# A hybrid decoder layer on one core: a hand-interleaved program is replaced by a recorded program that a list scheduler in the kernel's source lays out

## The chip, the core and the metric

The kernel runs on one core of a Trainium2 chip. The metric is device time of one execution in microseconds (us); less is better. The kernel before takes 591.33 us (median of three runs, 591.09 to 591.43).

A core has engines that each work through their own queue of instructions in order: TensorE (PE in the profile; its weight loads are PEld), VectorE (DVE), ScalarE (ACT), GpSimd (POOL), and SyncE (SP), which here issues all DMA transfers. They are tied together by semaphores. Matmuls write to PSUM, which has eight banks of 128 x 512 fp32; everything else lies in SBUF.

## The reference

One decoder layer, 1024 tokens of width 1024. The normed input is projected to 3584 columns that are split among eight stick-breaking attention heads (q, k, v), two blocks of a gated short convolution, four heads that attend to 256 memory tokens, and a gate over the whole mixing width.

```python
h = _rmsnorm(x, g_in); proj = h @ w_in
# stick-breaking: A[t,s] = sigmoid(z_ts) * prod_{s<j<t} (1 - sigmoid(z_tj))
z = einsum('bqhd,bkhd->bhqk', q_blk, k) * scale
log_not = where(before, log_sigmoid(-z), 0.0)
suffix = cumsum(log_not, axis=3, reverse=True) - log_not
w = where(before, exp(log_sigmoid(z) + suffix), 0.0)
y_sb = einsum('bhqk,bkhd->bqhd', w, v)
y_conv = b_c * causal_conv3(c_c * u_c)
y_mem = softmax(q_mem @ mk.T * scale) @ mv        # mk, mv from the normed memory
y = concatenate([_rmsnorm(y_sb), _rmsnorm(y_conv), _rmsnorm(y_mem)])
out = _rmsnorm(x + (y * silu(gate)) @ w_out)
```

## The kernel before, in words

Precision comes from splitting: each fp32 operand is written as a high part (`whi`, `xh`, `wth`, `q`) and a rest (`wlo`, `xl`, `wtl`, `qs`), and each product takes three (or two) fast matmuls. A split costs one cast and one subtraction.

**Start.** Lines 170 to 209 load x by chunks of 128 input channels, split it, and compute v of all heads in all eight PSUM banks at once (192 matmuls of 128 x 512). The row norms come out of the rows of x; v is copied to `vh`.

**Background work.** `proj` (line 267) projects one block of 128 columns: 48 matmuls of 128 x 512, 24 into each of two `pj` banks, one bank after the other, with a yield after every three. There are 24 such blocks, with the k and q of each head pair, the convolution, the memory queries and eight gates, and `mem_kv` (line 643) with 48 more matmuls. Weights come through one raw buffer `wraw` and two buffers each of `whi` and `wlo` (`load_w`, line 132): a DMA, two casts on ACT or DVE by the letters of `WENG`, two subtractions on POOL.

**A stick-breaking head.** Its queries are taken in four stages of 256 (`sp`). `sb_scores` (line 366) makes a block of scores z, takes two sigmoids of it on ACT (F, the chance of not breaking, and sg), runs a product scan over F on DVE (lines 387 and 389), and multiplies sg by F on DVE or POOL, as the letter of `MENG` says for that head (line 392): heads 0, 4, 5 and 7 on POOL, the others on DVE. `transposed` (line 331) transposes the weights on PE, casts them on ACT (`wth`, line 340) and subtracts on DVE (`wtl`, line 341); line 416 multiplies by v; `put_y` adds the halves. A head pair uses one q and one k projection (`qk`, two buffers). A memory head (`mem_unit`, line 508) has two such stages with a softmax in place of the scan.

**Order.** `attention` (line 681) lists the steps of six stick-breaking heads, then the four memory heads, then the last two stick-breaking heads. `run` (line 699) walks through them and, after each, advances the background until its time is the step's times a factor from `RATIO`; the order of the background is the string `BG` (line 50). `behind_attention` ties each third background matmul behind an attention step some places back. The program that comes out is ordered once more by the compiler's own scheduler, with a simulation of time.

**End.** The last gate (`proj_last`, line 251) uses the `z` banks. Then 8 blocks of 128 rows go through the output projection (line 789), three groups of PSUM pairs per block; the sum, the norm and the store follow on DVE, ACT and POOL.

Of the kernel before, what the change touches and what calls it, by code (L numbers as in the profile page):

```python
# [12 lines left out]

# [40 lines left out]
def hymba_kernel(ctx, tc, xT, xr, wp, wv, memT, memr, wmem, cols, eye, wout, gfin, out):  # L54
    nc = tc.nc
    PSUM = bass.MemoryType.PSUM

# [4 lines left out]
    vyp = ctx.enter_context(tc.tile_pool(name="vyp", bufs=1))
    ps_pj = ctx.enter_context(tc.tile_pool(name="ps_pj", bufs=PJ_BUFS, space=PSUM))
    ps_z = ctx.enter_context(tc.tile_pool(name="ps_z", bufs=2, space=PSUM))
    ps_tr = ctx.enter_context(tc.tile_pool(name="ps_tr", bufs=TR_BUFS, space=PSUM))
    ps_av = ctx.enter_context(tc.tile_pool(name="ps_av", bufs=2, space=PSUM))

    dram = ctx.enter_context(tc.tile_pool(name="dram", bufs=1, space=bass.MemoryType.DRAM))
    row = dram.tile([TB, P], F32, name="row")

    uid = [0]

    def nm(s):
        uid[0] += 1
        return f"{s}_{uid[0]}"

    def pj_tile():
        return ps_pj.tile([P, H], F32, tag="pj", name=nm("pj"))

    def z_tile():  # L80
        return ps_z.tile([P, H], F32, tag="z", name=nm("z"))

    def tr_tile():
        return ps_tr.tile([P, H], F32, tag="tr", name=nm("tr"))

    def av_tile(full=False):
        t = ps_av.tile([P, H], F32, tag="av", name=nm("av"))
        return t if full else t[:, 0:256]

    def stage(shape=None, dt=F32):  # L90
        return stg.tile(shape or [P, H], dt, tag="stg", name=nm("stg"))

    def slot(n, shape, dt, name):
        return vyp.tile(shape, dt, tag=f"s{n}", name=nm(name))
# [5 lines left out]
    col = const.tile([P, 32], F32, name="col")  # L100
# [9 lines left out]
    nhalf = const.tile([P, 8], F32, name="nhalf")  # L110
    nc.vector.memset(nhalf, -0.5)
    ones = const.tile([P, 2], F32R, name="ones")
    onesf = const.tile([P, 2], F32, name="onesf")
    nc.vector.memset(onesf, 1.0)
    nc.vector.tensor_copy(ones, onesf)
    rstd = const.tile([P, TB], F32, name="rstd")
    rq = const.tile([P, TB], F32, name="rq")
    nrq = const.tile([P, TB], F32, name="nrq")
    rb = const.tile([P, T], F32, name="rb")
    rstdm = const.tile([P, 2], F32, name="rstdm")  # L120
    rg = const.tile([P, 3, TB], F32, name="rg")
    sums = const.tile([P, TB], F32, name="sums")
    sumsm = const.tile([P, 2, 2], F32, name="sumsm")
    gsum = [const.tile([P, TB], F32, name=f"gsum{g}") for g in range(3)]

# [730 lines left out]
```

## Time and profile before

| | us |
|---|---|
| median of three runs | 591.33 |
| the profiled execution, its own time | 591.88 |
| its span on the core | 590.1 |
| start to the first score matmul of head 0 | 74.9 |
| heads 0 to 4 (to the first score matmul of head 5) | 178.1 |
| head 5 and the four memory heads | 107.2 |
| heads 6 and 7, last gates (to the first output matmul) | 133.8 |
| output projection to the last matmul | 89.7 |
| after the last matmul | 6.4 |

The profiled execution spends 1.8 us outside the span. The profile has a page (busy time of each engine, the chain of work that ended last, the costliest groups) and views of the trace: groups of instructions, stretches of time with each engine's busy time, and instructions in order of time. A matmul's end is modelled: it shows 0.39 us long although the next starts 0.23 us after it, so PE's busy share overstates its work; starts are the better measure.

### The profile page before, as it was taken

The page shows a single profiled execution, that of the slowest core. Times are in us where ns is not written, and L with a number is a line of the kernel's source. Part 1 is how long each engine was busy: PE and PEld are TensorE (multiplying, and loading weights), DVE is VectorE, ACT ScalarE, POOL GpSimd, SP SyncE. Part 2 cuts the span into 40 slices and gives each one's busy share as a digit, 9 for nine tenths or more (in the row PEclk, how much of TensorE's full clock was granted, in tenths as well). Part 3 has the DMA queues.
Part 4 walks back from the last instruction along what each step waited for, and adds up shares of the span by engine and source line. Part 5 has one row for each costly group of instructions (what it writes and reads, how often), then busy time and mean ns, then how long its engine had stood idle before and what let it go on. Part 6 is the DMA issues. An engine that isn't in the chain of part 4 may idle for free.

```text
span 590.1 us, 8309 instructions
## 1 busy us (share of the span) xinstructions
PE 556.6 (94%) x2776; PEld 460.2 (78%) x2776; DVE 426.6 (72%) x680; ACT 340.0 (58%) x743; POOL 300.5 (51%) x317
## 2 busy tenths in 40 slices
PE   8999999999899999978799999889988999999995
PEld 5888878878788888756688888778767878788884
DVE  3525039899999995779756858995887487977564
ACT  5747465657586686767556987554544464443332
POOL 2551586743134229987845667056876477301000
PEclk9999999999999999989899999889999999999999
DMA  8931421211312011232222221101001164132301
GB/s 284 403 137 38 116 64 36 73 37 36 108 37 72 24 49 37 55 90 72 71 83 66 69 72 36 37 36 37 30 7 36 37 252 142 37 142 103 113 37 71
DMA packets 22187, 48.36 MB, mean 82 GB/s; under 512 B 7808, under 2 KB 8320, under 8 KB 22144
## 3 DMA queue, kind: packets, MB, share of 16 engines
q1 hardware_dynamic: 22144, 47.82, 25.3%
q8 instruction: 22, 0.36, 0.2%
q14 instruction: 21, 0.17, 0.1%
HBM read 36.78 MB, written 4.20 MB: 69 GB/s over the span
## 4 chain that ended last, share of the span: by engine, by line
PE 32%; DVE 12%; issue 5%; ACT 3%; POOL 2%; DMA 2%; SPq 1%; POOLq 0%; DVEq 0%; ACTq 0%
PE pj L273 11%; PE tr L789 7%; PE pj L789 4%; PE z L789 3%; DVE wtl L341 2%; DVE F L389 2%; PE z L258 2%; DVE F L387 2%; PE tr L335 2%; PE av L416 1%; DMA part<-stg 1%; POOL sg L392 1%; PE z L527 1%; DVE whi L144 1%; DVE sg L392 1%
## 5 line engine op out<-in xcount | busy, mean ns | idle before, releaser
L273 PE MATMUL pj<-xh,whi 128*128 128x512 f32 x368 | 147.2, 400 | 1.0 <-DVE mv L668 1.0
L273 PE MATMUL pj<-xl,whi 128*128 128x512 f32 x368 | 145.1, 394 | 0.0
L273 PE MATMUL pj<-xh,wlo 128*128 128x512 f32 x368 | 145.1, 395 | 0.0
L145 POOL TENSOR_TENSOR wlo<-wraw,whi 128x512 fp32r<-128x512 f32 x56 | 82.6, 1491 | 26.3 <-ACT whi L142 12.9
L387 DVE TENSOR_TENSOR_SCAN F<-F,mask 128x513 f32<-128x513 f32 (+2 forms) x64 | 77.8, 1219 | 13.3 <-ACT F L384 10.0
L273 PEld LDWEIGHTS pj<-xh,wlo 128*128 128x128 f32 x368 | 69.3, 188 | 13.6
L273 PEld LDWEIGHTS pj<-xh,whi 128*128 128x128 f32 x368 | 69.4, 189 | 12.7 <-DVE mv L668 1.2
L273 PEld LDWEIGHTS pj<-xl,whi 128*128 128x128 f32 x368 | 69.6, 189 | 11.9
L392 POOL TENSOR_TENSOR sg<-sg,F 128x512 f32<-128x512 f32 (+3 forms) x48 | 62.2, 1298 | 27.6 <-DVE F L389 10.5
L384 ACT ACTIVATE F<-z,nrq 128x512 f32<-128x512 f32 (+3 forms) x96 | 56.1, 586 | 33.8 <-PE z L377 23.0
L341 DVE TENSOR_TENSOR wtl<-tr,wth 128x512 fp32r<-128x512 f32 (+1 forms) x96 | 59.7, 637 | 9.9 <-ACT wth L340 9.1
L385 ACT ACTIVATE sg<-z,rq 128x512 f32<-128x512 f32 (+2 forms) x96 | 55.7, 583 | 9.3 <-PE tr L335 9.2
L340 ACT CAST wth<-tr 128x512 fp32r<-128x512 f32 (+1 forms) x96 | 51.5, 555 | 14.9 <-PE tr L335 14.0
L416 PE MATMUL av<-wtl,vh 128*128 128x256 f32 (+1 forms) x160 | 43.3, 303 | 13.6 <-DVE wtl L341 13.5
L335 PE MATMUL tr<-ident,sg 128*128 128x128 f32 x288 | 48.3, 282 | 5.1 <-POOL sg L392 2.5
L383 POOL MEMSET F<- 128x1 f32 x96 | 9.8, 104 | 78.6 <-DVE F L389 38.8
L389 DVE TENSOR_TENSOR_SCAN F<-F,F,mask 128x512 f32<-128x512 f32 (+1 forms) x32 | 41.7, 1304 | 8.7 <-ACT F L384 6.4
L316 POOL TENSOR_TENSOR qs<-qk,q 64x512 fp32r<-64x512 f32 x24 | 32.7, 1377 | 28.7 <-ACT q L315 28.1
L416 PEld LDWEIGHTS av<-wtl,vh 128*128 128x128 f32 x160 | 31.3, 196 | 20.3 <-DVE wtl L341 18.0
L416 PE MATMUL av<-wth,vh 128*128 128x256 f32 (+1 forms) x160 | 45.1, 287 | 0.0
L801 POOL TENSOR_TENSOR ssf<-ssf,nhalf 128x1 f32<-128x1 f32 x8 | 7.4, 927 | 69.1 <-DVE ssf L798 59.8
L335 PEld LDWEIGHTS tr<-ident,sg 128*128 128x128 f32 x288 | 34.2, 144 | 9.2 <-POOL sg L392 3.9
(182 smaller groups left out, 1197.0 us busy)
## 6 DMA issues: line engine op xcount, KB each, us to landing
wraw<-in_wp SPq DMA_DIRECT2D x24, 512.0 KB, 3.3
xs<-in_xr SPq DMA_DIRECT2D x8, 512.0 KB, 7.9
wor<-in_wout SPq DMA_DIRECT2D x8, 512.0 KB, 4.9
acc<-in_xr SPq DMA_DIRECT2D x8, 512.0 KB, 3.8
out<-acc SPq DMA_DIRECT2D x16, 256.0 KB, 2.2
xs<-in_xT SPq DMA_DIRECT2D x7, 512.0 KB, 7.9
qs<-q SPq DMA_DIRECT2D x12, 256.0 KB, 2.9
q<-qs SPq DMA_DIRECT2D x12, 256.0 KB, 3.0
```

Source lines behind the costliest of these rows:

```text
L145: nc.gpsimd.tensor_tensor(lo[:, c], raw[:, c], f(hi[:, c]), op=ALU.subtract)
L273: ins = nc.tensor.matmul(ps, lhsT=ww[:, k, :], rhs=xx[k][:, hf], start=(k == 0 and a == 0), stop=(k == KC - 1 and a == 2))
L335: ins = nc.tensor.transpose(tr[:, i * P : (i + 1) * P], blk, ident)
L340: nc.scalar.copy(wh[:, 0:n], tr[:, 0:n])
L341: nc.vector.tensor_tensor(wl[:, 0:n], tr[:, 0:n], f(wh[:, 0:n]), op=ALU.subtract)
L384: nc.scalar.activation(F[:, 1:m], zz[:, 0 : m - 1], AF.Sigmoid, scale=nrq[:, i : i + 1])
L385: nc.scalar.activation(sg[:, c0:c1], zz, AF.Sigmoid, scale=rq[:, i : i + 1])
L387: nc.vector.tensor_tensor_scan(F[:, 0:m], F[:, 0:m], M[:, 0:m], 0.0, ALU.mult, ALU.max)
L389: nc.vector.tensor_tensor_scan(F[:, 0:m], F[:, 0:m], M[:, 130 : 130 + m], prev[:, H - lo : H - lo + 1], ALU.mult, ALU.max)
L392: eng.tensor_tensor(sg[:, c0:c1], sg[:, c0:c1], F[:, 0:w], op=ALU.mult)
L416: nc.tensor.matmul(av[:, 0 : c.stop - c.start], lhsT=key(j), rhs=w[:, c], start=(g == 0 and j == 1 and n == 0), stop=(g == ng - 1 and j == ...
L789: nc.tensor.matmul(ps[:, pc], lhsT=yy[:, c, :], rhs=ww[c][:, c0:c1], start=(c == cs[0] and a == 0), stop=(c == cs[-1] and a == 2))
```

## The change

Nothing of what is computed changes. The functions of the kernel no longer issue instructions: they record them in a `Plan`, which notes for each the tiles it reads and writes, so the instructions it must follow, and a priority. `lay_out` then plays the program on five engines with a table of costs, and at each moment gives every free engine the ready instruction of the lowest priority number whose tiles have room; `emit` issues them in that order, and the compiler's scheduler is switched off. Buffers of one tag are handed out in recorded order. Every instruction of the new program carries the line of the kernel's decorator, so its tiles tell them apart.

```diff
-WENG = 'vssssvvvsvvssvvsvvvssvvvvsss'
-MENG = 'pvvvppvp'
-KENG = 'ppvvvvvv'
-BG = 'qk1 c0 ms qk2 qm0 qm1 g0 kv qk3 g1 c1 g5 g7 g4 g6 g3 g2'
+COST = {"vector": (0.13, 0.00108), "scalar": (0.17, 0.00084), "gpsimd": (0.3, 0.0023)}
+LAG = {"tensor": 0.22, "vector": 0.1, "scalar": 0.1, "gpsimd": 0.12}
+PATIENCE = 6.0
...
+        def pick(e):
+            fits = [o for o in ready[e] if o.start is None and room(o)]
...
+            if e == "scalar":
+                same = [o for o in fits if o.table in (None, table)]
+                late = [o for o in fits if o.table not in (None, table) and now - o.ready > PATIENCE]
+                fits = late or same or fits
+            return min(fits, key=lambda o: (o.prio, o.n))
...
+    ATT, EVAC, SPLIT, FILL, POST = 1000.0, 300.0, 400.0, 5000.0, 20000.0
...
     def load_w(src, shape):
...
+            nc.scalar.copy(hi[:, c], raw[:, c], prio=SPLIT + fills[0])
+            nc.either.tensor_tensor(lo[:, c], raw[:, c], f(hi[:, c]), op=ALU.subtract, prio=SPLIT + fills[0])
...
+                nc.tensor.matmul(ps[i], lhsT=ww[:, k, :], rhs=xx[k][:, hf], start=first,
+                                 stop=(k == KC - 1 and a == 2), prio=FILL + fills[0] + (0 if both else 0.4 * i),
+                                 after=after if first else ())
...
-            eng = nc.vector if MENG[st["u"]] == "v" else nc.gpsimd
-            eng.tensor_tensor(sg[:, c0:c1], sg[:, c0:c1], F[:, 0:w], op=ALU.mult)
+            nc.either.tensor_tensor(sg[:, c0:c1], sg[:, c0:c1], F[:, 0:w], op=ALU.mult)
...
-    units = [(f"qk{p}", sb_unit(p, a, qk[p])) for p in range(3) for a in range(2)]
-    units += [("qm", mem_unit(h, qm, mkv)) for h in range(4)]
-    units += [("qk3", sb_unit(3, a, qk3)) for a in range(2)]
-    run(attention(units), bg, RATIO[0])
+    qk = [(q_proj(0), k_proj(4))]
+    pair(0, *qk[0])
+    qk.append((q_proj(1), k_proj(5)))
+    pair(1, *qk[1])
+    qk.append((q_proj(2), k_proj(6)))
+    conv(0)
+    pair(2, *qk[2])
+    qk.append((q_proj(3), k_proj(7)))
+    mk, mv = mem_kv()
+    stats(0, 0, True)
+    gate(0, (last[0],))
+    pair(3, *qk[3])
+    conv(1)
+    qm = [q_proj(14)]
+    mem_head(0, qm[0], mk, mv)
...
+    gate(6, (last[6],))
+    gate(7, (last[7],), both=True)
...
-    with tile.TileContext(nc, schedule_with_timeline_sim=True) as tc:
+    with tile.TileContext(nc) as tc:
```

`ATT` is the priority of attention (plus ten for each later head), `EVAC` that of emptying a projection's bank, `SPLIT` of splitting weights, `FILL` of projection matmuls, `POST` of the output. The lowest number goes first, so attention goes ahead of projections, and projections in recorded order take what is left. `either` lets VectorE or GpSimd take the instruction, whichever is free first. All eight stick-breaking heads now come before the memory heads. Pools, sizes and numbers of buffers are as before.

Three places show how instructions moved. On PE, at the start of head 5 of the kernel before (`z` scores, `av` times v, `tr` transposes, `pj` projections):

```order
L377 MATMUL z_2697<-k_2627,q_2619 128x512
L377 MATMUL z_2697<-k_2627,qs_2620 128x512
L416 MATMUL av_2539<-wth_2572,vh_464 128x256
L377 MATMUL z_2706<-k_2627,q_2619 128x512
L377 MATMUL z_2706<-k_2627,qs_2620 128x512
L416 MATMUL av_2539<-wtl_2573,vh_464 128x256
L416 MATMUL av_2539<-wth_2572,vh_464 128x256
L416 MATMUL av_2539<-wtl_2573,vh_464 128x256
L335 MATMUL tr_2653<-ident,sg_2503 128x128
L335 MATMUL tr_2653<-ident,sg_2579 128x128
```

The same place on PE after the change, in the first stage of head 5:

```order
L321 MATMUL z_2487<-k_2065,qs_2062 128x512
L321 MATMUL av_2367<-wtl_2478,vh_525 128x256
L321 MATMUL av_2508<-wth_2494,vh_525 128x256
L321 MATMUL pj_2388<-xl_241,whi_2140 128x512
L321 MATMUL pj_2514<-xh_160,whi_2328 128x512
L321 MATMUL av_2508<-wtl_2504,vh_525 128x256
L321 MATMUL pj_2388<-xh_232,wlo_2151 128x512
L321 MATMUL av_2508<-wth_2494,vh_525 128x128
L321 MATMUL tr_2526<-ident_151,sg_506_2420 128x128 x2
L321 MATMUL pj_2388<-xh_317,whi_2140 128x512
```

Before, the whole first stage of head 5 has no projection matmul; now they stand between the attention's, and the two banks of a block (here of two blocks) take turns.

On DVE before, in head 2, with the scans of F (shown under the name of their family, SCALAR_TENSOR_TENSOR) and the multiplies of sg:

```order
L389 SCALAR_TENSOR_TENSOR F_1480<-F_1480,F_1471,mask 128x512
L349 TENSOR_TENSOR y_682<-av_1332,avt_1379 64x256
L392 TENSOR_TENSOR sg_1467<-sg_1467,F_1471 128x512
L392 TENSOR_TENSOR sg_1467<-sg_1467,F_1480 128x512
L341 TENSOR_TENSOR wtl_1430<-tr_1424,wth_1429 128x512
L341 TENSOR_TENSOR wtl_1497<-tr_1492,wth_1496 128x384
```

On POOL after the change, in head 2:

```order
L321 TENSOR_TENSOR sg_268_1428<-sg_268_1428,F_1357 128x512
L321 MEMSET F_1473 128x1
L321 MEMSET F_1488 128x1
L321 TENSOR_TENSOR sg_273_1462<-sg_273_1462,F_1473 128x512
L321 MEMSET F_1514 128x1
L321 MEMSET F_1536 128x1
L321 TENSOR_TENSOR sg_292_1478<-sg_292_1478,F_1488 128x512
L321 TENSOR_TENSOR sg_297_1520<-sg_297_1520,F_1536 128x384
```

The multiplies of this head went from DVE to POOL. Over all heads POOL now does 77 of the 96 (48 before), DVE 19; in return 31 of the 56 subtractions of weight splits went from POOL to DVE, all 56 casts of weights are on ACT (30 were on DVE), and all subtractions for k on DVE (4 of 16 were on POOL).

On PE before, the last rows of the program, with the last two column blocks of the last 128 rows:

```order
L789 MATMUL tr_5815<-woh_5143,yh_5792 128x256
L789 MATMUL tr_5815<-wol_5144,yh_5792 128x256
L789 MATMUL tr_5815<-woh_5143,yl_5793 128x256
L789 MATMUL av_5874<-woh_5119,yh_5792 128x256
L789 MATMUL av_5874<-wol_5120,yh_5792 128x256
```

On PE after the change, the last rows:

```order
L321 MATMUL tr_5807<-woh_5136,yh_5673 128x256
L321 MATMUL av_5809<-woh_5136,yh_5673 128x256
L321 MATMUL tr_5807<-wol_5146,yh_5673 128x256
L321 MATMUL av_5809<-wol_5146,yh_5673 128x256
L321 MATMUL tr_5807<-woh_5136,yl_5686 128x256
L321 MATMUL av_5809<-woh_5136,yl_5686 128x256
```

Before, `tr` was complete twelve matmuls ahead of `av`; now the two end together.

More of the change, by code (lines that the diff above doesn't have):

```diff
@@ L12 @@
 from contextlib import ExitStack
-from itertools import chain
+import heapq
+import numpy as np
 import concourse.bass as bass
@@ L80, in z_tile @@
[L80 to L88, printed above, removed]
[L90 to L94 removed]
+    nc = Plan(ctx, tc)
@@ new lines, in hymba_kernel @@
+    const = Pool(nc, "const", {})
+    xpool = Pool(nc, "xpool", {"X": 16})
+    wring = Pool(nc, "wring", {"wraw": 1, "whi": 2, "wlo": 2})
+    stg = Pool(nc, "stg", {"stg": 6})
+    vyp = Pool(nc, "vyp", {"s4": 10})
+    att = Pool(nc, "att", {"qk": 2, "q": 2, "qs": 2, "k": 2, "sg0": 2, "sg1": 2, "F": 3, "wth": 3, "wtl": 3})
+    small = Pool(nc, "small", {"avt": 1, "mx": 2, "sm": 2, "part": 2})
+    psum = Pool(nc, "psum", {"pj": 2, "z": 2, "tr": 2, "av": 2}, space=PSUM)
+    dram = Pool(nc, "dram", {}, space=bass.MemoryType.DRAM)
@@ L96, in f, with bank, slot, one @@
+    dram.psum = False
+    row = dram.tile([TB, P], F32, "row")
+    def bank(tag):
+        return psum.tile([P, H], F32, tag)
+    def stage(shape=None, dt=F32):
+        return stg.tile(shape or [P, H], dt, "stg")
+    def slot(shape, dt, name):
+        return vyp.tile(shape, dt, "s4", name)
+    def one(shape, dt, name):
+        return const.tile(shape, dt, name, name)
     def f(ap):
         return ap.bitcast(F32)
-    col = const.tile([P, 32], F32, name="col")
+    col = one([P, 32], F32, "col")
@@ L105, in hymba_kernel @@
     cb = lambda cc: col[:, 30 + cc : 31 + cc]
-    M = const.tile([P, 642], BF16, name="mask")
-    ident = const.tile([P, P], F32, name="ident")
+    M = one([P, 642], BF16, "mask")
+    ident = one([P, P], F32, "ident")
     nc.vector.memset(M, 0.0)
[L110 to L124, printed above, removed]
+    nhalf = one([P, 8], F32, "nhalf")
+    ones = one([P, 2], F32R, "ones")
+    onesf = one([P, 2], F32, "onesf")
+    rstd, rq, nrq, sums = (one([P, TB], F32, n) for n in ("rstd", "rq", "nrq", "sums"))
+    rb = one([P, T], F32, "rb")
+    rstdm = one([P, 2], F32, "rstdm")
+    rg = one([P, 3, TB], F32, "rg")
+    sumsm = one([P, 2, 2], F32, "sumsm")
+    gsum = [one([P, TB], F32, f"gsum{g}") for g in range(3)]
+    ssf = one([P, TB, 4], F32, "ssf")
     def inv_rms(dst, src, width, n):
@@ L149, in row_stats @@
[L149 to L157 removed]
+    vps = [bank("pj"), bank("pj"), bank("z"), bank("z"), bank("tr"), bank("tr"), bank("av"), bank("av")]
     for _ in range(WARM):
@@ L520, in scores, with mem_head @@
+    def mem_head(h, qf, mk, mv):
+        unit[0] += 1
+        nc.prio = ATT + 10 * unit[0]
+        if h % 2 == 0:
+            new_y(6 + h // 2)
+        q, qs = q_stacks(qf, h % 2)
+        for tq in range(2):
+            nc.prio = ATT + 10 * unit[0] + tq
+            mx = small.tile([P, 4], F32, "mx")
+            sm = small.tile([P, 4], F32, "sm")
+            e = att.tile([P, 4, NMEM], F32, "sg0", "e")
             for t2 in range(2):
-                z = z_tile()
+                z = bank("z")
```

858 lines of the change are left out of this document (434 added, 424 removed).

## The prediction

> **What bounds the kernel now.** I read the page first, then stretches of time, then starts of instructions in order of time.
>
> ```profile
> PE 556.6 (94%) x2776; PEld 460.2 (78%) x2776; DVE 426.6 (72%) x680; ACT 340.0 (58%) x743; POOL 300.5 (51%) x317
> PE 32%; DVE 12%; issue 5%; ACT 3%; POOL 2%; DMA 2%; SPq 1%; POOLq 0%; DVEq 0%; ACTq 0%
> ```
>
> PE looks full at 94%, but its modelled ends overlap. Its work has to be counted by the spacing of starts where nothing makes it wait:
>
> ```profile
> 49.51 0.39 PE L273 MATMUL pj<-xh,whi 128*128 128x512 f32 x1
> ...
> 59.93 0.39 PE L273 MATMUL pj<-xl,whi 128*128 128x512 f32 x1
> 110.61 0.29 PE L416 MATMUL av<-wth,vh 128*128 128x256 f32 x1
> 110.73 0.29 PE L416 MATMUL av<-wtl,vh 128*128 128x256 f32 x1
> 110.86 0.60 PE L335 MATMUL tr<-ident,sg 128*128 128x128 f32 x4
> 111.21 0.36 PE L416 MATMUL av<-wth,vh 128*128 128x256 f32 x1
> 522.07 5.60 PE tr L789 x24
> ```
>
> 46 starts in 10.42 us make 0.227 for 128x512; in the attention it is 0.23, so I count 0.228. A 256-wide one takes 0.12, a transpose 0.0875 in a group of four (I count 0.095, since many stand alone), an output matmul 5.60/24 = 0.233. With the counts of the program's order this gives PE's work in each stage, to hold against the stage's length. The stages below are cut at the first score matmul of heads 0, 1, 5, 6 and 7 (for 7 it is 413.1), at the first output matmul (494) and behind the last matmul (583.7):
>
> ```profile
> core 0: us, PE busy (x) PEld busy (x) DVE busy (x) ACT busy (x) POOL busy (x), PEclk, DMA share, GB/s
> 0.00:74.90 74.90, 73.36 (x313) 58.23 (x314) 25.66 (x56) 43.51 (x85) 31.87 (x30) 1.00 0.55 193
> 74.90:108.10 33.20, 31.64 (x170) 26.77 (x169) 23.03 (x25) 20.60 (x41) 24.52 (x29) 1.00 0.18 52
> 108.10:253.00 144.90, 140.51 (x778) 119.74 (x777) 128.79 (x175) 96.71 (x195) 71.47 (x96) 1.00 0.18 52
> 253.00:360.20 107.20, 96.91 (x516) 80.96 (x516) 79.54 (x140) 75.23 (x175) 72.38 (x71) 0.97 0.27 74
> 360.20:413.10 52.90, 49.03 (x235) 40.93 (x234) 43.85 (x61) 30.56 (x60) 26.16 (x29) 0.94 0.12 36
> 413.10:494.00 80.90, 75.48 (x379) 61.49 (x378) 60.39 (x85) 40.33 (x89) 55.01 (x50) 1.00 0.21 72
> 494.00:583.70 89.70, 89.66 (x395) 72.05 (x393) 63.60 (x137) 31.83 (x99) 18.17 (x16) 1.00 0.27 94
> 583.70:590.10 6.40, 0.02 (x1) 0.00 (x0) 1.73 (x4) 1.23 (x3) 0.93 (x1) 0.90 0.22 82
> ```
>
> PE's work by count is 71.1, 30.5, 134.8, 88.9, 44.5, 72.1 and 87.7 us in the first seven: 529.6 together. The rest of the lengths is idle: 3.8, 2.7, 10.1, **18.3**, 8.4, 8.8 and 2.0, and 6.4 behind the last matmul. So 60 us of the span are not PE's work, and 27 of them lie between 253 and 413. There the order leaves PE without background work (head 5's first stage, shown above) and it waits for the chain through DVE:
>
> ```profile
> 261.39 0.58 PE L416 MATMUL av<-wtl,vh 128*128 128x256 f32 x1 [3.76 <-DVE wtl L341]
> 273.77 0.38 PE L416 MATMUL av<-wtl,vh 128*128 128x256 f32 x1 [1.38 <-DVE wtl L341]
> ```
>
> In heads 1 to 4 it is different: PE and DVE are both nearly full.
>
> ```profile
> 108.00:213.00 105.00, 101.09 (x566) 86.53 (x565) 100.63 (x143) 68.73 (x139) 37.60 (x60) 1.00 0.18 54
> ```
>
> DVE is busy 96% here. That balance is what the change must beat.
>
> **The change, term by term.** PE's work stays at 529.6: the same matmuls, moved. What can go is idle time. I sum the changed program by its own stages, from its order.
>
> *To the first score matmul.* 69.8 us of PE work, 1.3 less than before; with the same 3.8 of idle, 73.6. Row statistics are loaded earlier, and the memory pieces come later; behind 192 matmuls both are hidden. If that cover failed, a late x chunk would cost PE its wait, at most some 2 us.
>
> *Heads 0 to 6.* Between the first score matmuls of heads 0 and 7 stand 532 projection and memory matmuls (121.3), scores (30.0), 242 transposes and four more (23.4), 261 av matmuls (29.5) and four sums (0.9): PE 205 us. DVE's load uses these groups:
>
> ```profile
> L387 DVE TENSOR_TENSOR_SCAN F<-F,mask 128x513 f32<-128x513 f32 (+2 forms) x64 | 77.8, 1219 | 13.3 <-ACT F L384 10.0 <-POOL F L383 2.9
> L389 DVE TENSOR_TENSOR_SCAN F<-F,F,mask 128x512 f32<-128x512 f32 (+1 forms) x32 | 41.7, 1304 | 8.7 <-ACT F L384 6.4 <-POOL F L383 2.1
> L341 DVE TENSOR_TENSOR wtl<-tr,wth 128x512 fp32r<-128x512 f32 (+1 forms) x96 | 59.7, 637 | 9.9 <-ACT wth L340 9.1
> L392 DVE TENSOR_TENSOR sg<-sg,F 128x512 f32<-128x512 f32 (+3 forms) x48 | 34.5, 721 | 8.8 <-ACT sg L385 5.5
> L349 DVE TENSOR_TENSOR y<-av,avt 64x256 f32<-64x256 f32 x48 | 20.0, 416 | 8.4 <-ACT avt L348 7.8
> L300 DVE TENSOR_TENSOR k<-qk,k 64x512 fp32r<-64x512 f32 x12 | 9.4, 794 | 0.4
> L761 DVE TENSOR_TENSOR wol<-wor,woh 128x512 fp32r<-128x512 f32 x8 | 7.6, 957 | 0.6 <-ACT woh L760 0.6
> L639 DVE SCALAR_TENSOR_TENSOR stg<-stg,col,stg 128x256 fp32r<-128x256 f32 x8 | 6.4, 834 | 0.0
> L327 DVE TENSOR_TENSOR qk<-pj,rb 128x512 f32<-128x512 f32 x8 | 5.4, 676 | 17.1 <-PE pj L273 16.5 <-POOL qs L316 0.7
> ```
>
> 84 scans at 119.5/96 make 104.6; 69 wtl at 59.7/96, 42.9; 25 y halves, 10.4; 18 of the 84 multiplies, 13.0; 14 weight subtractions, which DVE did not do before, at the like L761's 0.957, 13.4; 12 for k, 9.5; 8 memory splits, 6.4; 14 bank evacuations at 0.68, 9.5; small ones about 10. The sum is 220; such sums of groups come out some 3% above the page's busy DVE, since neighbours overlap, so 213. DVE, not PE, is the larger load, by a little. At the 96% of the row above the seven heads take 222; at the 89% of heads 1 to 4 as a whole (128.79 of 144.9), 239. I take 93%: **230 us**. Outside bounds: PE alone at 96%, 214; and the pace of heads 0 to 4 before, (253.0 - 74.9)/5 = 35.6 a head, 249.
>
> *From head 7 to the last matmul.* PE work is 254.9. It is larger than before (159.8 from head 7 on) because the fill was saved up: about 14 blocks of projections are left, so PE has work without gaps. Idle: 4 in head 7, where DVE leads again; 2 around the memory heads; 2 in the output as before. Together 8, between 5 and 12. Work not needed on PE's path, the casts that moved to ACT (30 of L144's kind) among it, hides behind PE here: ACT was 58% busy. Without that cover it would join DVE's chain.
>
> *Tail.* The rows of before:
>
> ```profile
> 582.34 0.48 DVE L791 SCALAR_TENSOR_TENSOR acc<-tr,rg,acc 128x256 f32<-128x256 f32 x1 [0.68 <-PE tr L789]
> 583.44 0.28 PE L789 MATMUL av<-woh,yl 128*128 128x256 f32 x1
> 583.76 0.48 DVE L791 SCALAR_TENSOR_TENSOR acc<-av,rg,acc 128x256 f32<-128x256 f32 x1 [0.20 <-PE av L789]
> 584.28 0.42 ACT L794 ACTIVATE junk<-acc 128x256 f32<-128x256 f32 x1 [0.91 <-DVE acc L791]
> ```
>
> The tr piece is summed 1.4 us ahead of av. In the new order both end together, so one more addition (0.48) and square (0.42 and its read-out) stand behind the last matmul, with DVE's multiplication before them: +1.2, between 0 and 2. That makes 7.6.
>
> *Sum.* 73.6 + 230 + 254.9 + 8 + 7.6 = 574.1 span, and the 1.8 that lay outside it (591.88 - 590.1): 575.9, against 591.9 for the profiled execution. That execution stands 0.5 over the median, less than I can resolve: **576**.
>
> **A wait that the order makes likelier.** POOL now does 77 of the 96 multiplies, beside the scans. These rows show what that does:
>
> ```profile
> 151.73 1.28 DVE L389 TENSOR_TENSOR_SCAN F<-F,F,mask 128x512 f32<-128x512 f32 x1
> 258.41 1.26 POOL L392 TENSOR_TENSOR sg<-sg,F 128x512 f32<-128x512 f32 x1
> 258.73 2.03 DVE L389 TENSOR_TENSOR_SCAN F<-F,F,mask 128x512 f32<-128x512 f32 x1
> ```
>
> The same scan takes 1.28 alone and 2.03 when it starts 0.94 before POOL's multiply ends: it stands still nearly until POOL is done. [...]
>
> **The rivals.**
>
> 1. *The scans and POOL's multiplies exclude each other, and that sets the pace* (slower). The place is heads 0 to 6. For it: the three rows above, and heads 0 and 4, which multiplied on POOL, were no faster than the rest. Against it: what left DVE there were PE-bound heads (head 0: PE 30.5 of 33.2), and the 31 weight splits that left POOL pay part of it back. Price: 35.6 a head as before, 249 in place of 230, so 595. It decides from 35.1 us a head: (591.9 - 73.6 - 254.9 - 8 - 7.6 - 1.8)/7.
> 2. *PE becomes the only bound.* The planner fills every gap, heads 0 to 6 take 214: 560. For it: in the new order no stage of a head lacks projections. Against it: DVE's 213 leaves no slack at all.
> 3. *It does not do what it says at the end.* Both banks of a block advance by turns, so they end nearly together, and the next block waits for DVE's evacuation (0.68 and a hand-off of 0.2). Before, 24 matmuls of the other bank (5.5 us) hid this. Ten blocks outside the heads at 0.9 make 9: 585. Against it: in the order the turns slip apart by eight to twelve matmuls from block to block.
>
> **How the numbers follow.** Forecast 0.45 (its own range 566 to 586), rival 1 0.22, rival 2 0.18, rival 3 0.15. A measurement of this kernel can tell about 0.2%, 1.2 us, from no change. Faster by more: 0.45 + 0.18 + most of rival 3 and a little of rival 1, 0.75; within it 0.04; slower 0.21. The range of 8 in 10 reaches from rival 2's time to rival 1's: 560 to 595.
>
> **What would show it.** Right: the first score matmul near 74; head 7's near 304, with starts of heads 31 to 34 us apart and DVE at 93% between; no gap of PE over 1 us from head 7 to the end except at head 7; 7 to 8 us behind the last matmul. Rival 1 shows as scans whose mean goes over 1.4 us beside a fuller POOL; rival 2 as DVE under 90% and PE gapless; rival 3 as gaps of 0.5 to 1 us at the starts of blocks late in the program. I am wrong at the root if PE waits mostly for DMA or for POOL's weight splits, which I took as hidden.

## The result and the profile after

The changed kernel is slower: 614.34 us (median of four runs, 610.58 to 615.81) against 591.21 us beside it, a ratio of 1.0382 with a 95% interval of 1.0332 to 1.0431. The forecast was 576, its range 560 to 595. The profiled execution took 615.81 us, its span 614.0.

The two lines of the page that answer to those of before:

```profile
PE 569.6 (93%) x2776; PEld 458.2 (75%) x2776; DVE 427.1 (70%) x658; ACT 365.0 (59%) x777; POOL 287.3 (47%) x309
issue 2%; POOLq 0%; POOL 0%; ACT 0%; DVE 0%
```

The busy shares look as before, and the chain of waits breaks off 17 us from the end, so neither tells where 23 us went. The stages do. This is the same view of stretches as in the prediction, cut at the first score matmul of head 0, of head 6 and of head 7, at the first matmul of the memory heads, at the first output matmul, and behind the last one:

```profile
core 0: us, PE busy (x) PEld busy (x) DVE busy (x) ACT busy (x) POOL busy (x), PEclk, DMA share, GB/s
0.00:80.66 80.66, 76.36 (x307) 58.07 (x307) 32.87 (x61) 44.58 (x87) 23.37 (x23) 0.98 0.51 177
80.66:265.33 184.67, 179.00 (x1013) 151.17 (x1014) 165.31 (x206) 141.94 (x285) 117.97 (x151) 1.00 0.18 52
265.33:316.06 50.73, 41.80 (x200) 31.88 (x199) 41.07 (x55) 33.42 (x68) 29.43 (x33) 0.93 0.26 75
316.06:386.79 70.73, 68.17 (x348) 55.44 (x346) 41.28 (x56) 31.72 (x61) 33.96 (x36) 1.00 0.19 60
386.79:504.39 117.60, 110.61 (x515) 86.56 (x516) 73.00 (x139) 79.45 (x175) 65.77 (x54) 0.97 0.23 68
504.39:605.67 101.28, 93.70 (x399) 75.08 (x397) 70.64 (x138) 31.85 (x97) 15.92 (x14) 0.95 0.21 73
605.67:614.00 8.33, 0.01 (x1) 0.00 (x0) 2.89 (x7) 2.04 (x7) 0.92 (x1) 0.63 0.16 63
```

PE's work in them, counted as in the prediction (spacing of starts times the matmuls of the order), is 69.8, 169.3, 35.8, 64.8, 102.0 and 88.1 us. The rest of each length is idle time:

| stage | length | PE's work | idle | forecast of the idle time |
|---|---|---|---|---|
| start | 80.7 | 69.8 | 10.9 | 3.8 |
| heads 0 to 5 | 184.7 | 169.3 | 15.4 | 25 for heads 0 to 6 |
| head 6 | 50.7 | 35.8 | 14.9 | (in the line above) |
| head 7 and fill | 70.7 | 64.8 | 5.9 | 8 for all from head 7 to the last matmul |
| memory heads and last gates | 117.6 | 102.0 | 15.6 | (in the line above) |
| output | 101.3 | 88.1 | 13.2 | (in the line above) |
| tail | 8.3 | 0 | 8.3 | 7.6 |

Together 84.2 us are idle, against 60.5 before and 44.4 forecast. The largest shortfall is behind head 7: 34.7 where the forecast had 8.

Part of this idle time stands in the plan itself. `lay_out` needs no chip: run by itself on the kernel's source, it ends the plan at 574.7 us by its own prices (a computed length, not a measured one), with the matmuls in the order of the trace. That is next to the forecast's span of 574.1; the chip took 39.3 us more than the plan. By stages, plan and chip: start 74.4 and 80.7, heads 0 to 6 219.4 and 235.4, head 7 68.6 and 70.7, memory heads and last gates 116.2 and 117.6, output 89.0 and 101.3, tail 7.2 and 8.3. So the idle time of the memory heads (102.0 of work) was planned; that of the output was not.

What PE waited for, over the whole program, from the view of waits (in total, times, longest):

```profile
PE pj L321 <- DVE stg L321: 10.4, 6, 6.8
PE pj L321 <- ACT whi L321: 4.2, 1, 4.2
PE z L321 <- ACT e L321: 3.1, 1, 3.1
PE tr L321 <- POOL sg L321: 3.0, 3, 1.5
PE z L321 <- DMA q<-qs: 2.0, 1, 2.0
PE av L321 <- DVE wtl L321: 2.0, 4, 1.2
PE pj L321 <- ACT qk L321: 1.8, 1, 1.8
```

Before, the largest line there was DVE's `wtl`, in the attention (13.5 us in ten waits, the row of 3.76 us in the prediction among them); of that 2.0 are left. In its place are single long waits at hand-overs. All lines of that view add up to 34.7 us (26.9 before). Two other losses come on top. One is PE's clock, granted at half (the 0.50 in these lines) in four stretches; the first and third begin 0.46 and 0.59 us behind waits of 1.84 and 3.07 us, the second and fourth within waits of 4.20 and 6.76 us:

```profile
65.05:68.46 3.41, 3.41 (x10) 2.71 (x9) 0.69 (x1) 2.65 (x5) 2.33 (x2) 0.50 0.34 92
286.91:293.74 6.83, 3.89 (x9) 2.92 (x10) 6.31 (x9) 3.97 (x9) 3.88 (x6) 0.50 0.12 31
443.93:450.76 6.83, 6.58 (x22) 4.80 (x22) 3.85 (x7) 2.32 (x6) 2.37 (x3) 0.50 0.27 77
508.78:519.02 10.24, 5.69 (x13) 4.46 (x14) 9.35 (x9) 3.33 (x6) 5.05 (x4) 0.50 0.16 53
```

These four stretches hold 3.41 + 3.89 + 6.58 + 5.69 = 19.6 us of matmuls. A 128x512 matmul's start follows the last by 0.43 us in the first of them (65.67 to 66.10) and by 0.23 behind it (68.58 to 68.81), so I estimate that half of the 19.6, 9.8 us, would not be there at full speed. But the kernel before has such stretches too, four of 3.41 us (from 261.10, 284.99, 373.74 and 394.22), together:

```profile
sum 13.64, PE 12.97 PEld 11.60 DVE 12.04 ACT 4.22 POOL 8.97; mean PE 3.24 PEld 2.90 DVE 3.01 ACT 1.05 POOL 2.24
```

Half of 12.97 is 6.5, so by this estimate the change added only 3.3 us here. The other loss is small gaps: where one matmul's start lies 0.05 to 0.15 us later than the spacing of an unhindered one, these excesses add up to some 20.5 us (11.7 before). The added idle time is thus 7.8 us of waits, 3.3 of half clock, 8.8 of small gaps and 1.9 of tail, 21.8 of the 23.7: the small gaps weigh as much as the long waits.

The longest wait shows how it comes about. These are DVE's instructions at the start of the output (start, duration):

```profile
504.01 3.46 DVE L321 TENSOR_TENSOR wol<-wor,woh 128x512 fp32r<-128x512 f32 x2
507.39 1.35 DVE L321 TENSOR_TENSOR yl<-y,yh 128x128 fp32r<-128x128 f32 x1
508.67 4.01 DVE L321 TENSOR_TENSOR wol<-wor,woh 128x512 fp32r<-128x512 f32 x3
512.60 0.68 DVE L321 TENSOR_TENSOR stg<-pj,rb 128x512 f32<-128x512 f32 x1
```

and POOL's and PE's beside them:

```profile
502.39 7.47 POOL L321 TENSOR_TENSOR wol<-wor,woh 128x512 fp32r<-128x512 f32 x5
```

```profile
506.17 0.40 PE L321 MATMUL pj<-xh,wlo 128*128 128x512 f32 x1
513.33 0.79 PE L321 MATMUL pj<-woh,yh 128*128 128x512 f32 x1 [6.76 <-DVE stg L321]
```

PE finished the last gate at about 506.6 and next needs a `pj` bank. DVE's evacuation of that bank (`stg<-pj`, 0.68 us) stands behind five subtractions of output weights. The order has them there because, by the planner's prices, they were done before the gate was: the plan has the last of them end at 478.1 and the evacuation start at 478.5. It prices one at 0.79 us and knows nothing of POOL beside it. Here a subtraction takes up to 1.7 us while POOL does the same beside it, 0.69 and 0.68 just before POOL begins its own (at 500.83 and 502.11), and 0.68 at 513.20, where POOL is idle. So PE, DVE and the whole output stood behind work that could have waited.

In head 6 it is ACT (start, duration, wait):

```profile
285.91 1.12 ACT L321 CAST mk<-tr 64x256 fp32r<-64x256 f32 x3
288.26 0.37 ACT L321 CAST mk<-tr 64x256 fp32r<-64x256 f32 x1 [1.24 <-DVE mk L321]
288.66 0.63 ACT L321 ACTIVATE stg<-y 128x512 f32<-128x512 f32 x1
289.19 1.12 ACT L321 CAST whi<-wraw 128x512 fp32r<-128x512 f32 x2
```

PE's next matmul waits 4.2 us for `whi`, whose cast stands behind the casts of the memory keys and a square for the row sums. Most of this one is in the plan, which has PE idle for 3.6 us there. And it is DVE again at a sum that comes by DMA: a product that PE's transposes need, and an evacuation, stand behind `gsum`.

```profile
305.55 0.69 DVE L321 TENSOR_TENSOR wtl<-tr,wth 128x512 fp32r<-128x512 f32 x1 [0.22 <-ACT wth L321]
309.26 0.17 DVE L321 COPY gsum<-part 128x8 f32<-128x8 f32 x1 [3.02 <-DMA part<-stg]
309.35 0.69 DVE L321 TENSOR_TENSOR sg<-sg,F 128x512 f32<-128x512 f32 x1
309.95 0.68 DVE L321 TENSOR_TENSOR stg<-pj,rb 128x512 f32<-128x512 f32 x1
```

### The profile page after: what moved, and what is told of

Read it like the earlier page. It is cut to its first block, busy times and chain, and to the rows that moved or that the text cites. A ratio compares the mean times of both kernels' runs of the same rounds, so it can differ in the third digit from the quotient of the medians.

```text
span 614.0 us, 8204 instructions
## 1 busy us (share of the span) xinstructions
PE 569.6 (93%) x2776; PEld 458.2 (75%) x2776; DVE 427.1 (70%) x658; ACT 365.0 (59%) x777; POOL 287.3 (47%) x309
## 5 line engine op out<-in xcount | busy, mean ns | idle before, releaser
L321 PE MATMUL pj<-xl,whi 128*128 128x512 f32 x384 | 142.2, 402 | 0.0
L321 PE MATMUL pj<-xh,wlo 128*128 128x512 f32 x384 | 141.5, 400 | 0.0
L321 POOL TENSOR_TENSOR sg<-sg,F 128x512 f32<-128x512 f32 (+3 forms) x77 | 100.8, 1313 | 70.1 <-DVE F L321 59.4
L321 PEld LDWEIGHTS pj<-xh,whi 128*128 128x128 f32 x384 | 72.2, 191 | 31.4 <-DVE stg L321 7.6
L321 PEld LDWEIGHTS pj<-xh,wlo 128*128 128x128 f32 x384 | 72.7, 190 | 13.3
L321 POOL TENSOR_TENSOR wlo<-wraw,whi 128x512 fp32r<-128x512 f32 x25 | 36.6, 1467 | 53.0 <-ACT whi L321 53.0
L321 ACT CAST whi<-wraw 128x512 fp32r<-128x512 f32 x56 | 32.4, 618 | 40.8 <-PE pj L321 31.1
L321 POOL TENSOR_TENSOR stg<-stg,stg 128x512 f32<-128x512 f32 (+1 forms) x32 | 45.1, 1417 | 24.4 <-ACT stg L321 24.3
L321 PE MATMUL tr<-ident,sg 128*128 128x128 f32 x288 | 51.1, 276 | 4.7 <-POOL sg L321 3.0
L321 DVE TENSOR_TENSOR wlo<-wraw,whi 128x512 fp32r<-128x512 f32 x31 | 30.8, 1002 | 21.3 <-ACT whi L321 20.8
```

The source lines that it names most:

```text
L321: f(*[real(x) for x in o.args], **{k: real(x) for k, x in o.kw.items()})
```

## The experiments

Theory A: the order is fixed ahead from prices that are too low; where the real thing comes later, an engine stands behind one instruction with work ready behind it. Theory B: DVE and POOL lock each other, and their load is the loss. Theory C: the order of the big pieces (heads first, fill saved up) is the loss. Theory D: the turns between the two banks of a block are the loss. Ratios are to the kernel before on the same chip; the changed kernel has 1.0382.

**Single waits, and the order of the pieces.** The first run moves DVE's two evacuations of the last gate (kept in `early`) forward in the finished order:

```diff
+        for o in self.early:
+            order.remove(o)
+            order.insert(1 + max(order.index(self.ops[n]) for n in o.needs), o)
```

> The order as laid out, with one move: DVE's two evacuations of the last gate's banks are issued right behind their last matmul, so ahead of the output-weight subtractions that stand before them. Theory A (a fixed order, in which an engine stands behind one instruction that comes late): TensorE's wait of 6.76 us at 513 goes, and with it most of the half clock behind it (5.7 us at 0.5, so 2.8 us of work): 604 to 606 us. Theory B (DVE and POOL lock each other, and the load itself is too much there): the subtractions still take 1.7 us each, the first output matmuls wait for them instead, 611 to 613.

It took 613.77 us (1.0371, 1.0330 to 1.0413): nothing. But it was no test of A against B, for DVE's rows show the evacuation still behind three subtractions; the move passed only those that the order has behind the gate's last matmul.

```profile
509.37 2.95 DVE L329 TENSOR_TENSOR wol<-wor,woh 128x512 fp32r<-128x512 f32 x3
512.24 0.68 DVE L329 TENSOR_TENSOR stg<-pj,rb 128x512 f32<-128x512 f32 x1
```

The second takes the row sums off DVE's way; what adds them up (`late`), with the three inverse roots, is put behind the last evacuation:

```diff
-        part = small.tile([P, TB], F32, "part")
+        part = gsum[g] if first else small.tile([P, TB], F32, "part")
...
-        if first:
-            nc.vector.tensor_copy(gsum[g], part)
-        else:
-            nc.vector.tensor_tensor(gsum[g], gsum[g], part, op=ALU.add)
+        if not first:
+            nc.late.append(nc.vector.tensor_tensor(gsum[g], gsum[g], part, op=ALU.add))
...
+        order[at:at] = self.late
```

> The order as laid out, with the row sums of the groups taken off DVE's way: three of the four sums land by DMA where they are needed, without a copy, and the one addition and the three inverse roots are issued behind the last gate's evacuations. Theory A: DVE's four waits for these DMAs (3.0, 2.3, 1.2 and 5.5 us, 11.9 together) go; TensorE gets back what it waited behind them, 1.4 us at 311 and some 1 to 3 us near 424 to 500: 609 to 612 us. Theory B: DVE has slack there, nothing beyond 1 us: 613 to 615.

612.28 us (1.0337, 1.0307 to 1.0366), 0.3 above A's band and not apart from the changed kernel. DVE's 11.9 us of waits for the sums went; PE's wait at the output fell from 6.8 to 3.7 us, and a new one of 5.0 us came up behind it (ACT's `yh` of the last gate). A wait of DVE was worth little by itself.

The third has the memory heads between the third and the last pair, as before. It takes the row sums of the stick-breaking group after the gate of pair 2 has scaled that pair, so its output is another one; the instructions are the same.

> The same planner, with the pieces recorded in nearly the order of the kernel before: memory heads between the third pair and the last pair. Theory C (saving the background work for the end is what costs): faster than the changed kernel, 595 to 605 us, with the output ahead of 495. Theory A: the loss is in single waits, not in the order of the pieces; the last pair then lacks background work, 614 to 630 us.

633.22 us (1.0700, 1.0676 to 1.0724), 3 above A's band. Theory C falls: with nearly the old order of pieces the same planner loses 19 us more. That this is because the last pair then has little fill, and sums and gates come together at the end, is read from the order and not tried.

The fourth gives the casts of the next weights a better priority (`SPLIT` 200 for 400).

> The casts and subtractions of the next weights come ahead of evacuations in the planner's choice (200 for 400). Theory A: the wait of 4.2 us for ACT's cast at 290, behind the memory keys' casts, goes, and the 3.2 us of half clock work lost about it: 607 to 611 us. If the late piece there is not the cast but the ring of weights, or if evacuations now come late instead: 613 to 618.

615.68 us (1.0398, 1.0363 to 1.0433): the wait of 4.2 us for `whi` shrank to 0.95, and head 6 kept its length (50.5 us, from 267.1 to 317.6; 50.7 before the edit), with waits of 1.4 us and less. It came out as the second case of the expectation; what moved up in the wait's place was not traced further.

**The turns between banks.** The planner is told that a matmul may follow at once on the one before it (the second piece, of which the first line is shown, makes those that follow ready without the hand-off):

```diff
                     heapq.heappush(events, (end, o.n, o))
+                    if e == "tensor":
+                        heapq.heappush(events, (now + cost, -2 - o.n, (o,)))
...
+                if isinstance(o, tuple):
...
```

> The planner is told that a matmul may follow at once on the one before it in the same bank; the two banks of a block are then filled one after the other, and the first one's evacuation is hidden behind the second. Theory D (the banks' turns cost: rival 3 of the prediction): the wait of 1.84 us at 64.6 and the half clock behind it go (3.7 us together), and of the gaps of 0.05 to 0.15 us between TensorE's starts the 8 us that the change added: 601 to 606 us, first score matmul near 74 to 76. Without D: 612 to 616.

608.18 us (1.0273, 1.0244 to 1.0302), 6 us less, somewhat short of the band. The first score matmul stands at 74.6 us and the small gaps are 13.5 us in place of 20.5, both as expected by D. The wait for `qk` only fell from 1.84 to 1.58 us, and the large waits stayed: 6.7 us at the output. D is a part of the loss, about a quarter. The wait for `qk` is not D's: ACT's evacuation of the first block's bank stands behind its copies of `vh`, with the turns (first two rows) and without (last two):

```profile
63.18 0.37 ACT L321 ACTIVATE vh<-av,rstd 128x128 fp32r<-128x128 f32 x1 [0.42 <-DVE vh L321]
63.95 1.07 ACT L321 COPY qk<-pj 128x512 f32<-128x512 f32 x2
```

```profile
62.82 0.37 ACT L331 ACTIVATE vh<-av,rstd 128x128 fp32r<-128x128 f32 x1 [0.42 <-DVE vh L331]
63.09 0.58 ACT L331 COPY qk<-pj 128x512 f32<-128x512 f32 x1
```

**The last gate.** It gets the `z` banks, as it had before the change:

```diff
-        ps = [bank("pj"), bank("pj")]
+        ps = [bank(tag), bank(tag)]
...
-        proj(16 + c, evac, after, both)
+        proj(16 + c, evac, after, both, "z" if both else "pj")
```

> The last gate's two banks are taken from z in place of pj, so that the first output group (pj) needs neither of them; up to 414 us the order is the same. Theory A: the wait of 6.8 us for DVE's evacuation of pj and the half clock behind it (2.8 us) go, the output starts without a gap: 603 to 606 us. Theory B (the subtractions of the output weights on DVE and POOL, which lock each other, are the limit there): the output waits for them instead, 610 to 614.

603.75 us (1.0202, 1.0173 to 1.0232), as theory A has it. PE goes from the last gate into the output without a gap:

```profile
500.84 0.62 PE L321 MATMUL z<-xh,wlo 128*128 128x512 f32 x2
501.30 0.62 PE L321 MATMUL pj<-woh,yh 128*128 128x512 f32 x2
501.76 0.64 PE L321 MATMUL pj<-wol,yh 128*128 128x512 f32 x2
```

The subtractions are still there, but the output's first bank does not wait for them. One letter in the order of buffers was worth 10 us.

**DVE against POOL.** All 96 products of `sg` on DVE (`nc.vector` for `nc.either`):

> All 96 products of sg and F on DVE, none on POOL. Rival 1 of the prediction (scans and POOL's products exclude each other, so that it does not matter where a product stands): heads 0 to 6 take 230 to 240 us as in the changed kernel (235), 612 to 618 us in all, and the scans get shorter. If instead they overlap: DVE gets 66 more products of 0.72 in these heads, 47 us, of which at least half shows: heads 0 to 6 255 to 280 us, 630 to 655 in all.

631.63 us (1.0673, 1.0635 to 1.0711). Heads 0 to 6 took 264.5 us (78.7 to 343.1) in place of 235.4. The group of 64 of the 96 scans (the other 32 went from 1229 to 1040 ns) and the products, first of the changed kernel, then of this one:

```profile
L321 DVE TENSOR_TENSOR_SCAN F<-F,mask 128x513 f32<-128x513 f32 (+2 forms) x64 | 76.9, 1210 | 1.3 <-ACT F L321 1.1
```

```profile
L321 DVE TENSOR_TENSOR_SCAN F<-F,mask 128x513 f32<-128x513 f32 (+2 forms) x64 | 65.9, 1037 | 1.1 <-ACT F L321 0.6
L321 DVE TENSOR_TENSOR sg<-sg,F 128x512 f32<-128x512 f32 (+2 forms) x96 | 61.6, 651 | 0.4
```

Without POOL's products a scan takes 1.04 us in place of 1.21, so POOL's products do hold up the scans: 0.17 x 96 = 17 us of the program. But the 77 products that came to DVE cost 77 x 0.65 = 50. DVE gets two thirds of what POOL takes off it. Rival 1 (scans and products exclude each other, and that sets the pace) falls; that the scans take longer beside the products is real, at a third of the price: 17 of 50 us.

**Mends together.** Turns, sums and last gate:

> Three edits at once: no turns between a block's banks, no DMA sums on DVE's way, the last gate on z. If the losses are separate waits (theory A and D together): 608.2 less 9 for the last gate and less 2 for the sums, 595 to 599 us. If a mended wait only lets the next one come up: 603 to 608.

608.53 us (1.0279, 1.0254 to 1.0305): no better than the turns alone. POOL's and PE's rows show that my own edit did it; the three inverse roots, moved behind the last evacuation, stand ahead of the last gate's products on POOL, and PE waits for what follows from these:

```profile
502.91 4.85 POOL L336 TENSOR_TENSOR rg<-rg,nhalf 128x8 f32<-128x8 f32 x3 [1.51 <-DVE rg L336]
507.73 1.26 POOL L336 TENSOR_TENSOR wol<-wor,woh 128x512 fp32r<-128x512 f32 x1
508.94 2.48 POOL L336 TENSOR_TENSOR stg<-stg,stg 128x512 f32<-128x512 f32 x2
```

```profile
512.36 0.80 PE L336 MATMUL z<-woh,yh 128*128 128x512 f32 x1 [5.70 <-ACT yh L336]
```

It is theory A once more, made by hand. Without that edit, turns and last gate:

> The two edits that gained alone, together: no turns between a block's banks (608.2 alone) and the last gate on z (603.8 alone). If they are separate losses they add: 608.2 less the wait of 6.7 us and the 1.7 us of half clock at the output, 599 to 601 us. If the wait at the output only moves to the last gate's own chain (as with three edits, where ACT's yh came 5.7 us late behind three inverse roots on POOL): 606 to 609.

602.21 us (1.0170, 1.0135 to 1.0205), 1.2 above the band of separate losses, and it can't be told from the last gate alone (1.0202, 1.0173 to 1.0232); a wait of 2.4 us for the last gate's `yl` came up.

**The planner's prices.** On top of those two edits, first the DMA's prices, then the hand-off between engines:

```diff
-            o.cost = {engines[0]: 0.06}
+            o.cost = {engines[0]: 0.6 if o.nbytes < 4096 else 0.35}
...
-                        end = wire + 1.8
+                        end = wire + 3.0
```

```diff
-LAG = {"tensor": 0.22, "vector": 0.1, "scalar": 0.1, "gpsimd": 0.12}
+LAG = {"tensor": 0.5, "vector": 0.4, "scalar": 0.4, "gpsimd": 0.4}
```

> As the last, and the planner's prices of a DMA are those of the trace: an issue takes 0.35 us (0.6 for a column of sums) in place of 0.06, and its data come 3.0 us behind its turn on the wire in place of 1.8. Theory A (work that is planned for a time at which its data are not there): TensorE's waits for q<-qs (2.4 us at 74.6, 1.0 and 2.5 in the memory heads) go, and DVE's for the sums: 4 to 6 us less than the last. If these waits are the chain itself and not its place in the order: the same as the last within 1.5 us.

> As the last, and the planner's hand-off between engines is 0.4 to 0.5 us in place of 0.1 to 0.22, so that every order has slack. Theory A in its general form (the fixed order is too tight everywhere): TensorE's waits fall from 40 us to below 25, 585 to 594 us. If only the few named waits count, slack gains nothing and its longer chains lose: 597 to 606.

596.83 us (1.0086, 1.0060 to 1.0113) and 592.88 (1.0023, 1.0007 to 1.0039), both in the bands of theory A, the second at the upper end of its own. The sum of PE's waits fell from 32.3 us (turns and last gate, in its longest execution of 606.2) to 27.9 and to 23.0. With the DMA's prices DVE's waits for the sums went (6.2 us), those of PE for `q<-qs` only fell, from 6.6 to 3.0.

Which price was too low is another question. The DMA's issue was: four sums of 0.5 KB hold SP's queue for 2.41 us where the plan has 0.24 (first row, of SP's timeline in the changed kernel; the second is of its page, with the median from issue to landing).

```profile
490.24 2.41 SPq L321 DMA_DIRECT2D part<-stg  x4
part<-stg SPq DMA_DIRECT2D x32, 0.5 KB, 2.1
```

Its landing was not. The plan counts 0.3 us before the transfer, the transfer, and 1.8 behind it: 2.1 us for 0.5 KB and 2.8 for 256 KB. The page of the changed kernel has 2.1 from issue to landing for the first and 3.0 to 3.1 for the second (`qs<-q`, `q<-qs`). The 3.0 in the expectations is this whole time, not the part behind the transfer. Nor was the hand-off: in the prediction's rows of the tail DVE starts 0.04 us after PE's matmul ends, and ACT 0.04 after DVE. So 3.0 and 0.4 us are slack rather than prices, and these runs show that slack helps. Issue and landing were not raised one by one.

With the DMA's prices alone on the changed kernel, and then with slack in both (the hand-offs of DVE, ACT and POOL at 0.4, TensorE's left at 0.22, so that the turns stay):

> The changed kernel with the DMA's prices of the trace alone; hand-offs stay at 0.1. Slack in both gave 601.2. On top of the mends the DMA's share was 5.4 of 9.3 us: 606 to 609 us here if it is so in the changed kernel too; 612 to 616 if the hand-offs are what counts.

> The changed kernel with the planner's prices alone: a DMA as in the trace (0.35 or 0.6 us an issue, 3.0 us on its way), 0.4 us in place of 0.1 for a hand-off from DVE, ACT or POOL; the turns between banks and the last gate on pj stay. Theory A in its general form (hand-offs and DMAs priced too low are the cause): TensorE's waits fall by 10 us or more, the output's own wait stays: 597 to 605 us. If slack only helps once the turns and the last gate are mended: 610 to 616.

606.54 us (1.0252, 1.0231 to 1.0273) and 601.23 (1.0146, 1.0105 to 1.0188). Slack alone takes 13 us back, 8 of them the DMA's, with turns and last gate as they were. By its own prices the plan got longer by it, 590.6 us in place of 574.7; the span came down to 598.8, only 8.2 above its plan, where it had been 39.3. One part of the expectation was wrong, in A's favour: the wait at the output went too, from 6.76 to 0.75 us, although the last gate kept `pj`; with slack the order has the subtractions elsewhere. The engines' work stayed about the same (DVE busy 437.5 us in place of 427.1, POOL 278.3 in place of 287.3); what changed is the order.

**The sums in the memory heads.** An earlier place for memory keys and values first (`mem_kv` ahead of the last pair's projections, on top of the DMA's prices):

> As the one with the DMA's real prices, and the memory keys and values are recorded ahead of the last pair's projections. In the changed kernel head 6 is 15 us of idle TensorE beside them. If they are what leaves TensorE idle (both pj banks held until ACT and DVE are done with them) and an earlier place has more to cover it: heads 4 to 6 together 5 to 8 us shorter, 588 to 594 us. If the idle time moves with them: the same within 2 us.

598.02 us (1.0103, 1.0075 to 1.0131), the same within 2 us. Head 6 lost its idle time (15.2 to 1.7 us); heads 4 and 5 got it (4.4 to 15.5). The idle time goes where `mem_kv` goes. Then another order of recording behind head 7:

```diff
+    stats(4, 1, True)
     qm = [q_proj(14)]
...
-    stats(2, 0, False)
     last[6] = mem_head(1, qm[0], mk, mv)
     qm.append(q_proj(15))
-    gate(2, (last[2],))
-    stats(4, 1, True)
-    mem_head(2, qm[1], mk, mv)
     gate(4, ())
+    stats(2, 0, False)
+    mem_head(2, qm[1], mk, mv)
     gate(5, ())
+    gate(2, (last[2],))
```

> The kernel with slack, no turns and the last gate on z (592.9), and in its last part the row sums and gates of the convolution are recorded ahead of the memory heads, the sums of the last pair behind them: stages and the tr banks are given out in the order of recording, and there TensorE waits 4.1 us for ACT's stage at 433, beside 14 us of idle in the memory heads. If that order is the cause: the idle time of the memory heads falls to 5 to 8 us, 584 to 588 us, faster than before. If these sums wait wherever they stand: 591 to 595.

> The changed kernel with the other order of recording in its last part alone (sums and gates of the convolution ahead of the memory heads), with the prices, the turns and the last gate as they are. If the order of recording is a cause of its own: the idle time of the memory heads falls from 16 to some 8 us, 605 to 608 us. If it only shows once the prices leave slack (theory A): 611 to 616.

With slack, turns and last gate mended: **583.67 us** (0.9847, 0.9815 to 0.9880), faster than before. Alone on the changed kernel: 614.41 (1.0396, 1.0373 to 1.0420), nothing. The last stages of the fast one (cut as above: memory heads, output, tail):

```profile
376.36:482.24 105.88, 102.98 (x509) 84.41 (x508) 75.64 (x134) 72.58 (x166) 61.14 (x49) 1.00 0.27 87
482.24:575.23 92.99, 90.95 (x397) 72.52 (x395) 69.50 (x143) 31.28 (x99) 16.09 (x13) 1.00 0.19 69
575.23:581.80 6.57, 0.00 (x0) 0.00 (x0) 1.80 (x5) 1.23 (x3) 0.92 (x1) 0.86 0.21 80
```

The memory heads have 5.6 us of idle time (105.9 less 100.3 of work by count; 14.4 with slack and the old order), the output 5.5. The largest wait that went is shown here by PE's rows of the kernel with slack: a matmul for the row sums whose data are late, with the transposes of a head behind it.

```profile
428.30 0.39 PE L331 MATMUL tr<-stg,ones 128*2 128x512 f32 x1
432.83 0.59 PE L331 MATMUL tr<-stg,ones 128*2 128x512 f32 x1 [4.14 <-ACT stg L331]
```

This is not theory A's kind of wait: the plan itself has PE idle for 5.6 us there, as stages and banks are given out in the order of recording. With the other order the plan is 8.1 us shorter by its own prices (572.5 to 564.4), and the chip took 9.2 less. The plan could have told of this loss without a run.

## Why the prediction was wrong, point by point

**To the first score matmul: 73.6 forecast, 80.7.** PE's work (69.8) was right. The step that failed is "with the same 3.8 of idle": it was 10.9. ACT's evacuation of the first block stands behind the copies of `vh`, PE waits 1.84 us for it, and 3.4 us at half clock follow, which cost 1.7 by the estimate above; the rest of the 7.1 is smaller gaps. Before, the same evacuation came at 55.20, as soon as the bank was full. The turns are not the cause: without them PE waits 1.58 us there and the first score matmul stands at 74.6, but 5.0 of these 6 us are 22 matmuls that now come behind it.

**Heads 0 to 6: 230 forecast, 235.4.** The size was nearly right by luck, since two errors of the parts cancel. Heads 0 to 5 took 30.8 us each (forecast 32.9 on average; rival 2's pace is 30.6), with DVE busy 165.31 of 184.67 us, 90% and not 93%; PE's work is 92%, so DVE does not lead there. Over heads 0 to 6 DVE was busy 206.4 us where the sum has 213. Its step from 220 to 213, "some 3%", is shown nowhere: before, the groups of DVE add up to 452.6 us where the page has 426.6, 6%, and that gives 207. Head 6 took 50.7. What failed is "in the new order no stage of a head lacks projections", which I read from the counts of matmuls per head. Head 6 has them by count, but they could not run: PE is idle for 14.9 us there, 4.2 of them behind ACT's cast. By the order, both `pj` banks are held by the memory sums until ACT and DVE have emptied them, and weights come through one raw buffer; this is argued.

**From head 7 to the last matmul: 254.9 + 8 forecast, 254.9 + 34.7.** This is the step that turned the sign: an idle time of 8 us that was 34.7. "The fill was saved up, so PE has work without gaps" took for granted that work which is left is work that can run. PE goes through its queue in order; with fill behind it, it stood 6.76 us for a bank, 2.0 for a DMA (the plan has PE idle for less than 0.1 us before both) and 3.1 for a softmax (1.8 in the plan). The last two stretches of half clock cost 6.1 us by the same estimate. About 19 of the 34.7 us stand in the plan already (273.8 less 254.9); the forecast, which counted matmuls per stage, could not see them. What the runs put in its place: 10.6 us for the last gate's banks, 13 for the missing slack (the wait at the output, 6.76 to 0.75 us, is in both), 9 for the order of the sums once there is slack.

**Tail: 7.6 forecast, 8.3.** Right in its reason, short by 0.7: POOL's last root starts 2.8 us behind the last matmul in place of 1.3 (608.47 and 585.06), 1.5 more where 1.2 was forecast, and from there to the end it takes 0.5 us more.

**DVE and POOL.** That the two hold each other up was shown: a scan takes 1.21 us on average beside POOL's products and 1.04 with all of them on DVE, and in the kernel before a product of 128x512 on POOL takes 1.29 us at 79.41, where DVE is idle, and 2.18 at 89.57, beside a scan that DVE runs from 88.40 to 90.69. Rival 1 overstated the price of it, and the sum has it only as far as the groups of before do. In the heads the scans got no longer by it (means of 1.21 and 1.23 us, 1.22 and 1.30 before, far from the 1.4 that rival 1 asks for), but at the output, which the prediction did not look at, it made five subtractions take as long as eleven (3.46 + 4.01 us, at 0.68 each with POOL idle).

**The rivals.** Rival 3 named the turns between banks, at 9 us late in the program; they cost about 6, mostly in small gaps everywhere (20.5 to 13.5 us). Rival 1 had the sign right and the mechanism wrong. The case that happened was not among them: an order fixed ahead without slack. Two of its prices could be held against a trace: 0.06 us for a DMA's issue, where SP's rows have 0.33 us and 0.6 for a column of sums, and 0.79 us for a subtraction on DVE, which took 1.7 beside POOL. The half clock has no price in the plan at all. A list scheduler's order is only as good as these, and I summed the order as if each instruction met its data.

**What stays open.** Why the small gaps come with the turns was not tried by itself. Nor was which missing price the slack stands in for: a plan that knows of DVE and POOL holding each other up, or of the half clock, was not run. In head 6 the 15 us stay with `mem_kv` wherever it was put; that its two banks and its single raw buffer are the cause is argued from the order, not shown. And 84 us of idle time do not split into causes that add up: the mends overlap, since several take the same wait away.

## What to carry to other kernels

Before an order that is laid out ahead is believed, compare its prices with a trace: the DMA's issue (here 0.06 us against 0.33 to 0.6), and instructions that hold each other up (0.79 against 1.7), above all. Run the planner by itself and read its idle time and its length by stage, which costs nothing. Then give it slack: here 16 us more in the plan made the program 13 us shorter. Judge such a change by what stands directly ahead of each evacuation and each cast that PE needs, not by engine loads. When mends are tried one by one, expect some to show nothing until there is slack: the other order of the sums was worth 9 us with it and nothing without.

## What the runs showed of the hardware

PE's clock went to half after one wait of less than 2 us, of 1.84 us (62.75 to 64.59), but not after one of 2.03 us (384.76 to 386.79) in the same execution. Up to the last matmul the stretches at half are one, two, two and three times 3.41 us long (3.41, 6.83, 6.83, 10.24), and they start on one grid of this step: 65.05, 286.91, 443.93 and 508.78 are 221.86, 157.02 and 64.85 us apart, which is 65, 46 and 19 steps of 3.413. The wait of 1.84 us lies within one step of this grid (61.64 to 65.05). That of 2.03 us lies across its line at 385.90, with 1.14 us on one side and 0.89 on the other. So of these two waits the clock fell after the one that lay within one step, although it was the shorter. Two waits are few; what sets the grid, and how long a wait has to be, these runs do not show.
